# Where SiLU, sigmoid, relu and the squares stand in a group's stage, and a PSUM tile for each output step

## The chip, the cores and the metric

The kernel runs on one core of a Trainium2 chip. The metric is device microseconds (us) of one execution. Before the change the median of three runs is 1040.14 us (1040.02 to 1041.37).

## The reference

One layer of a hybrid trunk, with model width D = 1024, 512 tokens and 16 meta tokens ahead of them (L = 528):

```python
u = rmsnorm(h, mix_norm_w)
proj = u @ w_in                       # pooling, z, x/B/C, dt, gates
gate_pool, gate_ssd = sigmoid(proj[gates] + b_gate)
y_pool = pool_mixer(u_pool, pool_w_group, pool_scale) @ w_pool_up
# mamba2_branch, per group of 4 heads:
xbc = silu(conv4(xbc)); y = ssd_chunked(x, dt, a, B, C) + x * d_skip
y = y * silu(z)
y = y * rsqrt(mean(y * y over the group's 256 channels) + eps) * norm_w
y_ssd = y @ w_ssd_out
h = h + (gate_pool * y_pool + gate_ssd * y_ssd) @ w_o
v = rmsnorm(h, mlp_norm_w); h = h + relu(v @ w_ff1) ** 2 @ w_ff2
out = rmsnorm(h, final_norm_w)
```

The state-space branch has 8 groups of 4 heads, a head dimension of 64, a state of 128 and chunks of 128 tokens.

## The kernel before

All products keep fp32 accuracy by splitting each operand into a high and a low part: three matmuls per product (`mm3`, L99 to L101; the projections the same on L157, L158 and L160). Weights are streamed in blocks of 128 x 1024. For each block SP issues a load into `raw` (L74, three buffers), ScalarE (ACT) casts the high part `whi` (L75) and VectorE (DVE) subtracts to get the low part `wlo` (L76). `block()` returns the next block after it has issued this work for the blocks up to two further ahead, so a cast and a subtraction stand in the engines' queues at the place where the program asked for a block, two blocks before it is used.

The stages are: norm and first projections (to about 66 us), the groups' stage (to about 501 us), then pooling, gates, the output product W_o and the MLP. The change lies in the groups' stage, a loop over the 8 groups, in which PE, ACT and DVE run their instructions in the order in which the program writes them.

A group's cycle runs `Scan` for group g, interleaved with four steps of matmuls for the next group (`steps`): its projections B, C, x0, x1, each followed on ACT and DVE by a convolution over four taps (one pass on ACT, L347, three on DVE, L350). For group 4 the steps are instead eight output steps (`out_half`, tiles `pso`, copied to `acc` by ACT at L590), over the first eight of the normed outputs `ys`; group 4's own four projections come after them. For group 7 they are eight output steps `out_part` (tiles `psp`, added to `acc` by DVE, L598). The parts of a scan, in order:

- turn: transposes of B (tile `ptb`, L424), of x's meta tokens (`ptm`, L433) and of x (`ptx`, L444) on PE; from them ACT makes `bm` and `btok` (L428 to L430) and DVE `xdm`, `xm`, `xdt`, the low part of `bm` (L449) and `xdd` (L450);
- spread: `eb`, an Exp on ACT (L457); spans: four relus per head on `abc` (L463); decays: Exp on half of `abc` (L468);
- states: products `pcb` (L475) and `pst` (L482, L484), and the recurrence over chunks on DVE;
- scores: `abc` times `cbm` on DVE (L493); outputs: `po` (L503) and `py` (L509);
- gather: `yt` from `po`, `py`, x and z's SiLU `zt` on DVE;
- squares: Square on ACT (L522), the sum of two halves on DVE (L523), and high and low part of it (L249, L250); norm: `png` (L529); root: Ln and Exp on ACT (L533, L534); finish: `yt` scaled on DVE (L539), its high part on ACT (L542), its low part on DVE (L543).

After the scan come the next group's z in two halves (`z_half`, tile `pz`), the SiLUs of B, C and x (L354) and of z (L672), and, after groups 1, 2, 3 and 6, the product of one further pooling gate (`gate_pool`, tile `pgp`) and its sigmoid (L556). PSUM has a pool of two tiles of two banks each, used in turn by `px`, `pz`, `pgp`, `pso` and `psp`, and a pool of four single banks for the scan's small products. A tile can be taken again once its last reader is done. ACT holds one table set of functions at a time, and an `ACT_TABLE_LOAD` stands where the set changes: Ln, Exp, SiLU and sigmoid follow one another with loads between them.

Of the kernel before, what the change touches and what calls it, by code (L numbers as in the profile page):

```python
# [11 lines left out]
AF = mybir.ActivationFunctionType  # L12
ALU = mybir.AluOpType
# [3 lines left out]
SEQ = 512  # L17
NM = 16
L = SEQ + NM
HALF = L // 2  # L20
NK = D // P
# [14 lines left out]
V_MIX, V_BG, V_PS, V_CW, V_CB, V_DS, V_SN, V_MN, V_DTB, V_AL = (  # L36
    0, 8, 24, 32, 160, 192, 208, 224, 232, 233)
# [14 lines left out]
def kernel(ctx: ExitStack, tc, xT, x, w, vec, fnw, out):  # L52
    nc = tc.nc
    act, dve, pe, pool = nc.scalar, nc.vector, nc.tensor, nc.gpsimd
# [26 lines left out]
    def block():  # L81
        prepare(depth[0] + 1)
        return ahead.pop(0)[2:]

    def prepare(n):
        while len(ahead) < n:
            ahead.append(block_tiles())
            block_part(ahead[-1], slice(0, 1024))
# [32 lines left out]
    def col(off, i, n=P):  # L121
        return vs[:n, off + i : off + i + 1]
# [22 lines left out]
    m1 = [m1p.tile([P, SEQ], F32, tag=f"m1_{d}", name=f"m1_{d}") for d in range(NK)]  # L145

    def psum2(name):
        return psa.tile([P, 1024], F32, tag="mm", name=name)

    def psum1(name):  # L150
        return psb.tile([P, 512], F32, tag="s", name=name)

    def proj_step(outs, k, wblk, rhs):

        wh, wl = (t[:, k * P : (k + 1) * P] for t in wblk)
        for o, c in outs:
            pe.matmul(o, wh, rhs[0][k][:, c], start=k == 0, stop=False)  # L157
            pe.matmul(o, wh, rhs[1][k][:, c], start=False, stop=False)  # L158
        for o, c in outs:
            pe.matmul(o, wl, rhs[0][k][:, c], start=False, stop=k == NK - 1)  # L160

    def proj(outs, wblk, rhs):
        for k in range(NK):
            proj_step(outs, k, wblk, rhs)
# [8 lines left out]
    def narrow(ps):  # L173
        return [(ps, slice(NM, L))]
# [8 lines left out]
    rsb = pre.tile([P, L], F32, name="rsb")  # L183
    q = pre.tile([P, L], F32, name="q")
    X, U = (xh, xl), (uh, ul)
# [81 lines left out]
    for t, name in ((rsh, "dgh"), (rsl, "dgl")):  # L267
        d = pre.tile([NT, 6, NT], F32R, tag="sq", name=name, bufs=2)
# [84 lines left out]
    def silu(t):  # L353
        act.activation(t, t, AF.Silu)  # L354

    def group_tiles(g):
        xc = gc.tile([P, 2, L], F32, tag="xc", name=f"xc{g}")
        bt = gc.tile([P, L], F32, tag="bt", name=f"bt{g}")
        ct = gc.tile([P, SEQ], F32, tag="ct", name=f"ct{g}")
        zt = gc.tile([P, 2, SEQ], F32, tag="zt", name=f"zt{g}", bufs=1)  # L360
        return xc, bt, ct, zt
# [28 lines left out]
    def xbc_tile(g, cur, n):  # L390
        dst, t, skip = tiles_of(g, cur)[n]
        runs, view = wide(psum2(f"px{g}_{t}"), skip)
        proj(runs, block(), U)
        return lambda: conv(dst, view, t)

    def z_half(ps, i, between=None):
        wblk = block()
        for k in range(NK):
            if k == 2 and between:
                between()  # L400
            proj_step(narrow(ps[:, i * SEQ : (i + 1) * SEQ]), k, wblk, U)
# [146 lines left out]
    flat = lambda t: t.rearrange("p r d -> p (r d)")  # L548


    def gate_pool(d, first=False):
        ps = psum2(f"pgp{d}")[:, :SEQ]
        proj(narrow(ps), block(), X if first else U)
        if first:
            dve.tensor_tensor(m1[d], ps, rsb[:, NM:], op=ALU.mult)
        act.activation(m1[d], m1[d] if first else ps, AF.Sigmoid, bias=col(V_BG, d))  # L556


    cur = group_tiles(0)
    first_group(cur)  # L560
    for d in range(GATES_FIRST):
        gate_pool(d, True)
    depth[0] = 2
    prepare(2)
    norm_u()
# [11 lines left out]
    def ssd_out(d, ps, ks):  # L577
        wh, wl = block()
        for n, k in enumerate(ks):
            c = slice(n * P, (n + 1) * P)  # L580
            mm3(ps, (wh[:, c], wl[:, c]), ys[k], n == 0, n == len(ks) - 1)

    half = {}

    def out_half(d):
        if d % 2 == 0:
            half[0] = psum2(f"pso{d}")
        ps = half[0][:, (d % 2) * SEQ : (d % 2 + 1) * SEQ]
        ssd_out(d, ps, range(8))
        return lambda: act.copy(acc[d], ps)  # L590

# [2 lines left out]
    def out_part(d):  # L594
        ps = psum2(f"psp{d}")[:, :SEQ]
        for k in range(8, 14):
            mm3(ps, next(part), ys[k], k == 8, k == 13)
        return lambda: dve.tensor_tensor(acc[d], acc[d], ps, op=ALU.add)  # L598

    def scan_with(sc, steps):  # L600
        sc.turn()
        after = steps[0]()
        sc.spread()
        sc.spans((0, 1))
        after()
        sc.states()
        after = steps[1]()
        sc.decays(0)
        sc.spans((2,))
        after()  # L610
        after = steps[2]()
        sc.spans((3,))
        sc.decays(1)
        sc.scores(0)
        sc.scores(1)
        after()
        sc.outputs()
        after = steps[3]()
        sc.gather(0)
        if len(steps) > 4:  # L620
            after()
            after = steps[4]()
        sc.gather(1)
        if len(steps) > 4:
            sc.squares()
        after()
        if len(steps) > 4:
            steps[5]()()
            sc.norm()
            after = steps[6]()  # L630
            sc.root()
            after()
            after = steps[7]()
            sc.finish()
            after()

    with tc.manual_schedule(engines={mybir.EngineType.PE, mybir.EngineType.Activation, mybir.EngineType.DVE}):
        for g in range(G):
            sc = Scan(g, cur)
            if g + 1 == G:  # L640
                scan_with(sc, [lambda d=d: out_part(d) for d in range(NK)])
                break
            nxt = group_tiles(g + 1)
            tiles = [lambda n=n: xbc_tile(g + 1, nxt, n) for n in range(4)]
            if g == 4:
                scan_with(sc, [lambda d=d: out_half(d) for d in range(NK)])
                for t in tiles:
                    t()()
            else:
                scan_with(sc, tiles)  # L650
            gate = GATE_AT.get(g)
            xc, bt, ct, zt = nxt
            ps = psum2(f"pz{g + 1}")
            z_half(ps, 0)

            def silus():
                for t in (bt, ct, xc.rearrange("p i t -> p (i t)")):
                    silu(t)

            if g == 4:  # L660
                silus()
                z_half(ps, 1)
            else:
                sc.squares()
                if gate is None:
                    silus()
                z_half(ps, 1, sc.norm)
                sc.root()
                sc.finish()
                if gate is not None:  # L670
                    silus()
            act.activation(zt.rearrange("p i t -> p (i t)"), ps, AF.Silu)  # L672
            if gate is not None:
                gate_pool(gate)
            cur = nxt
    depth[0] = 0
    gc_stack.close()
# [49 lines left out]
    def gate_ssd(d):  # L727
        ps = psum1(f"pgs{d}")
        proj(narrow(ps), block(), U)
        gt = gtp.tile([P, SEQ], F32, tag="gt", name=f"gs{d}")  # L730
        act.activation(gt, ps, AF.Sigmoid, bias=col(V_BG, NK + d))
        return gt
# [4 lines left out]
    for d in range(NK):  # L737
        ps = psum2(f"psl{d}")[:, :SEQ]
# [4 lines left out]
    for n, gi in enumerate(POOL_ORDER):  # L743
        nxt = []
        if n < 3:
            nxt.append(pool_tile(2 * POOL_ORDER[n + 1]))
        if n == 0:
            gate_pool(NK - 1)
        if n == 3:
            gts = [gate_ssd(MERGE[0])]  # L750
        if n == 2:
            wgb = block()
        pool_mix(gi, pend, wgb)
        if n < 3:
            nxt.append(pool_tile(2 * POOL_ORDER[n + 1] + 1))
        pend = nxt
# [79 lines left out]
    first = []  # L836
    for n, d in enumerate(MERGE):
# [6 lines left out]
        ps = psum2(f"pup{d}")[:, :SEQ]  # L844
# [303 lines left out]
    for t in range(4):  # L1148
        T, st = t // 2, slice((t % 2) * P, (t % 2 + 1) * P)
        n = 0  # L1150
        for half in range(2):
            parts = [(0, 512)] if half == 0 or t < 3 else [(0, 256), (256, 256)]
            for a, m in parts:
                ps = p2v[t] if T == 0 and half == 0 else lastp[:, 512:] if a else (
                    lastp[:, :512] if (t, half) == (3, 0) else psum1(f"pl{t}_{half}"))
                ps = ps[:, a : a + m]
                i = 0
                for k, seg in ((1, (A11, 3)[T]), (0, (A12, A22)[T])):
                    wh, wl = wq[k, half]
                    for p in range(2):  # L1160
                        x0 = p * 512 + a
                        f = i == 0 and not (T == 0 and half == 0)
# [152 lines left out]
```

## Time and profile before

| | us |
|---|---|
| median of three runs | 1040.14 |
| the profiled execution | 1041.51 |
| its span | 1039.8 |
| its mean granted TensorE clock | 0.993 of full speed |
| groups' stage, about | 66 to 501 |

A row of the waits names the engine and tile that waited, the line, the engine and line that ended the wait, and then the total, the number and the longest wait in us. A row of the windows gives a stretch of the span in us, its length, the busy time of PE, of its weight loads, of DVE, ACT and POOL (instructions in brackets), the granted clock of PE, the DMA share and GB/s. A row of the timeline gives start, length, engine, line, operation, output and inputs, and in square brackets how long the engine had been idle and what ended that. In the chain that ended last a row has start, length, engine, tile and line. A row of the DMA issues ends with the us from issue to landing. A row of a tile gives its instructions by count, min/median/max ns and the first and the last start.

### The profile page before, as it was taken

To read this page: it belongs to the slowest core of one execution; us is meant where nothing else is said; L and a number is where in the kernel's file an instruction comes from. 1 tells how busy PE (TensorE), PEld (TensorE's weight loads), DVE (VectorE), ACT (ScalarE), POOL (GpSimd) and SP (SyncE) were. 2 spreads that over 40 slices of the span, in tenths; PEclk is the share of its full clock that TensorE was granted. 3 is DMA by queue.
4 is the path that set the end of the run, shared out by engine and by line. 5 is a ranking of instruction groups with operands and counts; after the bars stand their busy time and mean duration, and the time that the engine had idled before them with its cause. 6 is when DMAs were issued, how large, how long until landed. Compare 5 with 4: busy or idle time off the path is not lost.

```text
span 1039.8 us, 14039 instructions
## 1 busy us (share of the span) xinstructions
PE 1012.1 (97%) x5689; PEld 875.9 (84%) x5689; DVE 711.3 (68%) x894; ACT 559.9 (54%) x789; POOL 88.6 (9%) x52
## 2 busy tenths in 40 slices
PE   9999999999889999999999999999999999999997
PEld 8889889898678998978899888888888888888886
DVE  7979585858453486767757457885777666666866
ACT  7774949494734467575344333465455344454444
POOL 0100000000000000000000000101231412403400
PEclk9999999999999999999999999999999999999999
DMA  6233131414232322322723332414323323234112
GB/s 235 81 124 110 53 124 59 142 42 142 61 105 78 102 83 80 122 61 81 238 87 101 102 102 71 152 55 169 101 81 122 101 83 120 88 115 116 44 44 82
DMA packets 29282, 105.64 MB, mean 102 GB/s; under 512 B 3296, under 2 KB 4256, under 8 KB 28192
## 3 DMA queue, kind: packets, MB, share of 16 engines
q1 hardware_dynamic: 26496, 92.75, 27.7%
q0 software_dynamic: 2000, 11.08, 2.9%
q8 instruction: 45, 0.74, 0.3%
q10 hardware_dynamic: 720, 0.91, 0.2%
q14 instruction: 21, 0.17, 0.1%
HBM read 102.55 MB, written 2.16 MB: 101 GB/s over the span
## 4 chain that ended last, share of the span: by engine, by line
PE 75%; DVE 12%; ACT 10%; issue 1%; DMA 0%; SPq 0%; DVEq 0%; ACTq 0%
PE pf L100 6%; PE pf L101 6%; PE pf L99 6%; PE alpha L1064 3%; PE alpha L1065 3%; PE alpha L1066 3%; PE px L157 3%; PE px L158 3%; PE px L160 3%; DVE wlo L76 2%; PE pp L157 1%; PE pp L160 1%; PE pp L158 1%; PE pgs L160 1%; PE pup L101 1%
## 5 line engine op out<-in xcount | busy, mean ns | idle before, releaser
L76 DVE TENSOR_TENSOR wlo<-raw,whi 128x1024 fp32r<-128x1024 f32 (+1 forms) x131 | 163.8, 1252 | 127.4 <-ACT whi L75 127.4
L75 ACT CAST whi<-raw 128x1024 fp32r<-128x1024 f32 (+1 forms) x131 | 136.2, 1041 | 126.6 <-PE pf L100 55.8
L157 PE MATMUL px<-uh,whi 128*128 128x264 f32 (+1 forms) x448 | 121.1, 291 | 0.0
L158 PE MATMUL px<-ul,whi 128*128 128x264 f32 (+1 forms) x448 | 118.0, 285 | 0.0
L99 PE MATMUL pf<-vh,whi 128*128 128x512 f32 x256 | 99.8, 390 | 0.0
L101 PE MATMUL pf<-vh,wlo 128*128 128x512 f32 x256 | 99.6, 389 | 0.0
L100 PE MATMUL pf<-vl,whi 128*128 128x512 f32 x256 | 99.6, 389 | 0.0
L160 PE MATMUL px<-uh,wlo 128*128 128x264 f32 (+1 forms) x448 | 90.9, 284 | 0.0
L157 PEld LDWEIGHTS px<-uh,whi 128*128 128x128 f32 x448 | 85.6, 191 | 1.3 <-issue 1.0
L158 PEld LDWEIGHTS px<-ul,whi 128*128 128x128 f32 x448 | 85.1, 190 | 0.3
L826 DVE TENSOR_TENSOR slo<-b,shi 128x1024 fp32r<-128x1024 f32 x35 | 49.2, 1405 | 31.6 <-ACT shi L825 27.4
L160 PEld LDWEIGHTS px<-uh,wlo 128*128 128x128 f32 x448 | 69.2, 189 | 0.0
L825 ACT CAST shi<-b 128x1024 fp32r<-128x1024 f32 x35 | 36.8, 1051 | 47.3 <-PE pf L100 36.4
L99 PEld LDWEIGHTS pf<-vh,whi 128*128 128x128 f32 x256 | 48.1, 188 | 10.0
L101 PEld LDWEIGHTS pf<-vh,wlo 128*128 128x128 f32 x256 | 48.1, 188 | 10.0
L100 PEld LDWEIGHTS pf<-vl,whi 128*128 128x128 f32 x256 | 48.1, 188 | 9.9
L1075 POOL TENSOR_TENSOR b<-b,b 128x1024 f32<-128x1024 f32 x14 | 35.6, 2540 | 238.4 <-DVE slo L826 238.4
L1064 PE MATMUL alpha<-shi,hh 128*128 128x512 f32 x140 | 54.6, 390 | 0.0
L1066 PE MATMUL alpha<-shi,hl 128*128 128x512 f32 x140 | 54.5, 389 | 0.0
L1065 PE MATMUL alpha<-slo,hh 128*128 128x512 f32 x140 | 54.5, 389 | 0.0
L891 DVE TENSOR_TENSOR ht<-ht,alpha 128x1024 f32<-128x1024 f32 x35 | 42.6, 1217 | 10.9 <-PE alpha L1066 10.9
L347 ACT ACTIVATE xc<-px,vs 128x528 f32<-128x528 f32 x14 | 11.1, 791 | 70.9 <-PE px L160 70.9
(415 smaller groups left out, 2519.3 us busy)
## 6 DMA issues: line engine op xcount, KB each, us to landing
raw<-in_w SPq DMA_DIRECT2D x129, 512.0 KB, 3.6
b<-in_w SPq DMA_DIRECT2D x28, 512.0 KB, 3.5
abc<-acs_d POOLq DMA_DIRECT2D x8, 1024.0 KB, 5.3
wob<-in_w SPq DMA_DIRECT2D x8, 512.0 KB, 5.4
xt<-in_xT SPq DMA_DIRECT2D x8, 264.0 KB, 5.6
ht<-in_x POOLq DMA_DIRECT2D x4, 512.0 KB, 6.0
w<-in_w SPq DMA_DIRECT2D x4, 512.0 KB, 3.6
out_dram<-out SPq DMA_DIRECT2D x4, 320.0 KB, 2.4
```

Of the source, the lines that this page charges most:

```text
L75: act.copy(hi[:, c], raw[:, c])
L76: dve.tensor_tensor(lo[:, c], raw[:, c], hi[:, c].bitcast(F32), op=ALU.subtract)
L99: pe.matmul(ps, ah, bh, start=first, stop=False)
L100: pe.matmul(ps, ah, bl, start=False, stop=False)
L101: pe.matmul(ps, al, bh, start=False, stop=last)
L157: pe.matmul(o, wh, rhs[0][k][:, c], start=k == 0, stop=False)
L158: pe.matmul(o, wh, rhs[1][k][:, c], start=False, stop=False)
L160: pe.matmul(o, wl, rhs[0][k][:, c], start=False, stop=k == NK - 1)
L826: dve.tensor_tensor(lo, src, hi.bitcast(F32), op=ALU.subtract)
L1064: pe.matmul(ps[t], a[0], wh[:, cs], start=f, stop=False, skip_group_check=True)
L1065: pe.matmul(ps[t], a[0], wl[:, cs], start=False, stop=False, skip_group_check=True)
L1066: pe.matmul(ps[t], a[1], wh[:, cs], start=False, stop=l, skip_group_check=True)
```

## The change

Six things change, all in the groups' stage.

1. The squares of a group are issued in the scan directly behind the last convolution; before, they stood behind z's first half, or in groups 4 and 7 ahead of a step's copy.
2. The SiLUs of B, C and x always stand ahead of z's second half's products in the program; before, in the groups with a gate, they stood behind finish.
3. z's SiLU: in groups with a gate it stands directly behind z's second half, ahead of Ln, Exp and finish; in the others it is put on the list `held` and issued in the next scan behind its turning.
4. The gate's sigmoid is held in the same way. Its product stays where it was on PE.
5. The eight relus of heads 0 and 1 go from behind `eb` to behind the states and step 1's matmuls.
6. Each output step `out_half` takes a PSUM tile of its own; before, two steps shared one, each with one bank. In groups 4 and 7 the last step's copy or addition stands ahead of finish.

The diff:

```diff
-    def gate_pool(d, first=False):
+    def gate_product(d, rhs=U):
         ps = psum2(f"pgp{d}")[:, :SEQ]
-        proj(narrow(ps), block(), X if first else U)
-        if first:
-            dve.tensor_tensor(m1[d], ps, rsb[:, NM:], op=ALU.mult)
-        act.activation(m1[d], m1[d] if first else ps, AF.Sigmoid, bias=col(V_BG, d))
+        proj(narrow(ps), block(), rhs)
+        return ps
...
-    half = {}
-
     def out_half(d):
-        if d % 2 == 0:
-            half[0] = psum2(f"pso{d}")
-        ps = half[0][:, (d % 2) * SEQ : (d % 2 + 1) * SEQ]
+        ps = psum2(f"pso{d}")[:, :SEQ]
         ssd_out(d, ps, range(8))
         return lambda: act.copy(acc[d], ps)
...
+    held = []
+
     def scan_with(sc, steps):
         sc.turn()
         after = steps[0]()
+        while held:
+            held.pop()()
         sc.spread()
-        sc.spans((0, 1))
         after()
         sc.states()
         after = steps[1]()
+        sc.spans((0, 1))
         sc.decays(0)
         sc.spans((2,))
         after()
...
         sc.gather(1)
-        if len(steps) > 4:
-            sc.squares()
         after()
+        sc.squares()
         if len(steps) > 4:
             steps[5]()()
             sc.norm()
             after = steps[6]()
             sc.root()
             after()
-            after = steps[7]()
+            steps[7]()()
             sc.finish()
-            after()
...
             z_half(ps, 0)
-
-            def silus():
-                for t in (bt, ct, xc.rearrange("p i t -> p (i t)")):
-                    silu(t)
-
-            if g == 4:
-                silus()
-                z_half(ps, 1)
+            for t in (bt, ct, xc.rearrange("p i t -> p (i t)")):
+                silu(t)
+            z_half(ps, 1, None if g == 4 else sc.norm)
+
+            def z_silu(zt=zt, ps=ps):
+                act.activation(zt.rearrange("p i t -> p (i t)"), ps, AF.Silu)
+
+            if gate is not None:
+                z_silu()
+                pg = gate_product(gate)
             else:
-                sc.squares()
-                if gate is None:
-                    silus()
-                z_half(ps, 1, sc.norm)
+                held.append(z_silu)
+            if g != 4:
                 sc.root()
                 sc.finish()
-                if gate is not None:
-                    silus()
-            act.activation(zt.rearrange("p i t -> p (i t)"), ps, AF.Silu)
             if gate is not None:
-                gate_pool(gate)
+                held.append(lambda d=gate, pg=pg: act.activation(m1[d], pg, AF.Sigmoid, bias=col(V_BG, d)))
             cur = nxt
```

The gates outside this stage do what they did (product, then sigmoid). What the order of instructions shows at three places:

On ACT at the end of group 2's cycle, from Ln to the end of the SiLUs (`rs` is root's tile, `yh` finish's high part, `bt`, `ct`, `xc` and `zt` group 3's B, C, x and z), before:

```order
L533 ACT_TABLE_LOAD
L533 ACTIVATE rs_2190<-png_2169,eps 128x512
L534 ACT_TABLE_LOAD
L534 ACTIVATE rs_2190<-rs_2190 128x512
L542 CAST yh_0_2194<-yt_2023 128x512
L542 CAST yh_1_2199<-yt_2023 128x512
L354 ACT_TABLE_LOAD
L354 ACTIVATE bt_1763<-bt_1763 128x528
L354 ACTIVATE ct_1764<-ct_1764 128x512
L354 ACTIVATE xc_1762<-xc_1762 128x1056
L672 ACTIVATE zt_1765<-pz_2119 128x1024
L75 CAST whi_2209<-raw_2208 128x1024
```

The same stretch after the change, on ACT:

```order
L354 ACTIVATE bt_1762<-bt_1762 128x528
L354 ACTIVATE ct_1763<-ct_1763 128x512
L354 ACTIVATE xc_1761<-xc_1761 128x1056
L75 CAST whi_2161<-raw_2160 128x1024
L661 ACTIVATE zt_1764<-pz_2126 128x1024
L75 CAST whi_2196<-raw_2195 128x1024
L533 ACT_TABLE_LOAD
L533 ACTIVATE rs_2225<-png_2172,eps 128x512
L534 ACT_TABLE_LOAD
L534 ACTIVATE rs_2225<-rs_2225 128x512
L542 CAST yh_0_2229<-yt_2023 128x512
L542 CAST yh_1_2234<-yt_2023 128x512
```

The four SiLUs and the gate block's cast have moved from behind finish's casts to ahead of Ln.

On ACT directly behind that, group 3's turning and its first steps (`m_4` is the gate, `abc` the spans' tile, `st_3` the first state), before:

```order
L556 ACT_TABLE_LOAD
L556 ACTIVATE m_4_126<-pgp_2207,vs 128x512
L428 CAST bm<-ptb_2248 16x128
L429 CAST bm<-ptb_2248 16x128
L430 COPY btok_2247<-ptb_2248 128x384
L75 CAST whi_2280<-raw_2279 128x1024
L457 ACT_TABLE_LOAD
L457 ACTIVATE eb_2333<-abc_2239 64x1024 x2
L463 ACTIVATE abc_2239<-abc_2239,dtok 128x128 x8
L347 ACTIVATE bt_2242<-px_20_2278,vs 128x528
L486 COPY st_3_2355<-pst_0_2359 128x256
L75 CAST whi_2374<-raw_2373 128x1024
```

And after the change, the same place on ACT:

```order
L428 CAST bm<-ptb_2247 16x128
L429 CAST bm<-ptb_2247 16x128
L430 COPY btok_2246<-ptb_2247 128x384
L75 CAST whi_2279<-raw_2278 128x1024
L672 ACT_TABLE_LOAD
L672 ACTIVATE m_4_126<-pgp_2194,vs 128x512
L457 ACT_TABLE_LOAD
L457 ACTIVATE eb_2333<-abc_2238 64x1024 x2
L347 ACTIVATE bt_2241<-px_20_2277,vs 128x528
L486 COPY st_3_2347<-pst_0_2351 128x256
L75 CAST whi_2366<-raw_2365 128x1024
L463 ACTIVATE abc_2238<-abc_2238,dtok 128x128 x8
```

The sigmoid with its load has moved from ahead of the turning's copies to behind the next cast, and the eight relus from ahead of the first convolution pass to behind the state's copy and a cast.

On PE in group 4, from the end of output step 0 to the first matmul of step 1 (`yh3_1` is the last of the normed outputs used, `wlo37` and `whi38` blocks of weights, `xdd4` and `btok4` made by the turning), before:

```order
L101 MATMUL pso0_2757<-yh3_1_2678,wlo37_2638 128x512
L475 MATMUL pcb4_2800<-ct4_2243,bt4_2242 128x128 x4
L482 MATMUL pst4_0_2811<-xm_115,bm_114 128x256
L484 MATMUL pst4_0_2811<-xdd4_2754,btok4_2726 128x256
L484 MATMUL pst4_1_2812<-xdd4_2754,btok4_2726 128x256 x2
L99 MATMUL pso0_2757<-yh0_0_1271,whi38_2688 128x512
```

After the change, the same place on PE:

```order
L101 MATMUL pso0_2756<-yh3_1_2713,wlo37_2641 128x512
L475 MATMUL pcb4_2792<-ct4_2242,bt4_2241 128x128 x4
L482 MATMUL pst4_0_2803<-xm_115,bm_114 128x256
L484 MATMUL pst4_0_2803<-xdd4_2753,btok4_2725 128x256
L484 MATMUL pst4_1_2804<-xdd4_2753,btok4_2725 128x256 x2
L99 MATMUL pso1_2816<-yh0_0_1271,whi38_2675 128x512
```

The order is the same; step 1's first matmul writes `pso1` where it wrote into the second half of `pso0`.

More of the change, by code (lines that the diff above doesn't have):

```diff
@@ L548, with gate_first @@
     flat = lambda t: t.rearrange("p r d -> p (r d)")
-    def gate_pool(d, first=False):
+    def gate_product(d, rhs=U):
         ps = psum2(f"pgp{d}")[:, :SEQ]
-        proj(narrow(ps), block(), X if first else U)
-        if first:
-            dve.tensor_tensor(m1[d], ps, rsb[:, NM:], op=ALU.mult)
-        act.activation(m1[d], m1[d] if first else ps, AF.Sigmoid, bias=col(V_BG, d))
+        proj(narrow(ps), block(), rhs)
+        return ps
+    def gate_first(d):
+        ps = gate_product(d, X)
+        dve.tensor_tensor(m1[d], ps, rsb[:, NM:], op=ALU.mult)
+        act.activation(m1[d], m1[d], AF.Sigmoid, bias=col(V_BG, d))
     cur = group_tiles(0)
@@ L561 @@
     for d in range(GATES_FIRST):
-        gate_pool(d, True)
+        gate_first(d)
     depth[0] = 2
@@ L747 @@
         if n == 0:
-            gate_pool(NK - 1)
+            pg = gate_product(NK - 1)
+            act.activation(m1[NK - 1], pg, AF.Sigmoid, bias=col(V_BG, NK - 1))
         if n == 3:
```

## Prediction

> **What bounds the kernel now.** I read the page's head first, then the waits of TensorE, then the windows in which its clock falls, and last the timeline of a group.
>
> ```profile
> span 1039.8 us, 14039 instructions
> PE 1012.1 (97%) x5689; PEld 875.9 (84%) x5689; DVE 711.3 (68%) x894; ACT 559.9 (54%) x789; POOL 88.6 (9%) x52
> PE pso L99 <- ACT acc L590: 7.0, 3, 3.3
> PE py L509 <- DVE abc L493: 3.9, 4, 1.1
> PE pst L482 <- DVE bm L449: 3.3, 2, 1.6
> PE ptm L433 <- ACT xc L354: 2.4, 4, 0.6
> PE pst L484 <- DVE xdd L450: 1.9, 3, 0.6
> PE png L529 <- DVE qlg L250: 0.9, 4, 0.2
> ```
>
> PE is busy for 97%, so a change that leaves its matmuls alone can win only PE's waits and what they cause. The six rows (us in total, times, longest) are all in the groups' stage; their sum is 7.0 + 3.9 + 3.3 + 2.4 + 1.9 + 0.9 = 19.4 us. They cause something more:
>
> ```profile
> 120.81:124.22 3.41, 3.41 (x16) 3.23 (x15) 0.00 (x0) 3.36 (x8) 0.00 (x0) 0.50 0.45 154
> 277.82:281.23 3.41, 3.41 (x10) 2.62 (x9) 3.11 (x6) 2.60 (x6) 0.00 (x0) 0.50 0.00 0
> 308.54:311.95 3.41, 3.41 (x9) 2.65 (x8) 1.23 (x1) 0.36 (x1) 0.00 (x0) 0.50 0.11 24
> 410.94:414.35 3.41, 1.74 (x13) 1.36 (x11) 3.22 (x8) 3.36 (x7) 0.00 (x0) 1.00 0.00 0
> 414.35:417.76 3.41, 2.80 (x7) 2.29 (x8) 1.60 (x2) 3.35 (x4) 0.00 (x0) 0.50 0.16 24
> ```
>
> The first number after the length is PE's busy time, the 0.50 or 1.00 the granted clock. Four windows ran at half clock, in groups 1, 4 (twice) and 6, and did 1.7 us of work in 3.41: each costs about 1.6. The one at 414.35 followed a window in which PE was busy for 1.74 of 3.41 us.
>
> An undisturbed group is group 0; against it stands group 2, whose turning follows a gate's product:
>
> ```profile
> 66.44 0.49 PE L424 MATMUL ptb<-ident,bt 128*128 128x128 f32 x3
> 74.79 1.46 PE L484 MATMUL pst<-xdd,btok 128*128 128x256 f32 x6
> 89.50 1.97 PE L509 MATMUL py<-abc,xdt 128*64 128x128 f32 x32
> 108.71 0.49 PE L424 MATMUL ptb<-ident,bt 128*128 128x128 f32 x3
> L157 PE MATMUL pgp<-uh,whi x8: 389/389/389, 157.3 to 162.1; 128*128 128x512 f32 x8
> 162.78 0.49 PE L424 MATMUL ptb<-ident,bt 128*128 128x128 f32 x3
> 163.85 1.00 ACT L672 ACTIVATE zt<-pz 128x1024 f32<-128x1024 f32 x1
> 214.38 1.00 ACT L672 ACTIVATE zt<-pz 128x1024 f32<-128x1024 f32 x1
> ```
>
> From a turning PE needs 8.35 us to the states (74.79 - 66.44), 23.06 to py and 42.27 to the next turning. A gate's product adds 5.44 (157.34, in the timeline, to 162.78), so 47.71 is a gate group without a wait. Group 2's cycle, from zt to zt, takes 50.53: 2.8 too long. The waits in it are ptm 0.6, py 1.0 and png 0.2; the other 1.0 is slower matmuls behind them.
>
> **The change part by part.** PE's instructions keep number and order; only the PSUM tile of every second output step is another. Table loads on ACT stay 46. So everything is a shift of ACT and DVE work, and the sum is over PE's waits.
>
> *A gate group (2 and 3).* Before, silus of bt, ct and xc stand behind finish, and xc's ends after PE wants it (ptm). Now they stand in z's second half, so ptm's wait goes. What is late next is finish, since z's SiLU now stands ahead of Ln. The rows for its chain:
>
> ```profile
> 154.37 0.69 ACT L533 ACTIVATE rs<-png,eps 128x512 f32<-128x512 f32 x1
> 156.37 0.63 ACT L534 ACTIVATE rs<-rs 128x512 f32<-128x512 f32 x1
> 157.04 0.75 DVE L539 SCALAR_TENSOR_TENSOR yt<-yt,vs,rs 128x512 f32<-128x512 f32 x1 [2.72 <-ACT rs L534]
> 160.53 0.69 DVE L543 TENSOR_TENSOR yl<-yt,yh 128x512 fp32r<-128x512 f32 x1 [0.69 <-ACT yh L542]
> 164.75 1.03 ACT L75 CAST whi<-raw 128x1024 fp32r<-128x1024 f32 x1
> 165.80 1.28 ACT L556 ACT_TABLE_LOAD   x1
> 167.10 0.69 ACT L556 ACTIVATE m<-pgp,vs 128x512 f32<-128x512 f32 x1
> 166.96 0.41 DVE L434 TENSOR_TENSOR xdm<-ptm,decm 16x256 f32<-16x256 f32 x1
> 170.11 0.96 DVE L450 TENSOR_TENSOR xdd<-xdt,dec 128x768 f32<-128x768 f32 x1
> 465.25 0.97 DVE xdd L450
> 466.36 1.53 PE pst L484 x6
> ```
>
> Count from the end of z's product, which is the gate product's start. z's SiLU starts at about 0.2; the cast + 0.90 (163.85 to 164.75), the table load + 1.05, Ln + 1.30 (like 165.80 to 167.10): 3.45. Exp + 2.00 (154.37 to 156.37), yt + 0.67, last yl + 3.49 and 0.61 for itself: 10.2. From xdm to xdd 3.15: 13.4; the states' product 1.11 behind (465.25 to 466.36): 14.5. PE is there at 5.44 + 8.35 = 13.8. A new wait of **0.7**, then.
>
> The scores come after. ACT ends the last yh at 9.6; the turning's small copies (an estimate: 1.0) and the next cast (1.03) go to 11.6, and two loads (1.28 each) with the held sigmoid (0.69) put eb at 14.9:
>
> ```profile
> 170.94 2.14 ACT L457 ACTIVATE eb<-abc 64x1024 f32<-64x1024 f32 x2
> 173.10 2.45 ACT L463 ACTIVATE abc<-abc,dtok 128x128 f32<-128x128 f32 x8
> 176.27 2.37 DVE L350 SCALAR_TENSOR_TENSOR bt<-px,vs,bt 128x527 f32<-128x527 f32 x3 [4.06 <-ACT bt L347]
> 183.04 2.32 DVE L350 SCALAR_TENSOR_TENSOR ct<-px,vs,ct 128x512 f32<-128x512 f32 x3
> 186.40 2.35 DVE L493 TENSOR_TENSOR abc<-abc,cbm 128x1024 f32<-128x1024 f32 x2
> ```
>
> Without the eight relus (2.45, moved behind the states) bt's conv starts on ACT 2.16 after eb, at 17.0, and DVE's passes 0.8 later, as 173.10 + 2.45 stands to 176.27. The scores come 10.13 behind those (186.40 - 176.27): 28.0, their first half at 29.1. PE wants it at 5.44 + 23.06 + 0.7 = 29.2. So py's wait goes or shrinks to 0.25. The relus are hidden in C's step: between 17.0 and DVE's turn to ct's conv (6.77 behind bt's, at 24.6) ACT now has bt's pass 0.8, st's copy 0.4 (an estimate), a cast 1.0, eight relus 2.45, an Exp of a cast's size, 1.1, four relus 1.2 and ct's pass 0.7, together 7.65, to 24.65: no slack. If that cover is gone, each 0.1 missing there is 0.1 of py's wait. Squares sooner make png's wait go. Cycle: 47.71 + 0.7 + 0.1 = 48.5; gain 2.0 each, **3.9** for both. At the bounds: no new wait 2.8 each; or, if each of the three hand-overs on the new chain costs another 0.6 (ptm's wait), 0.2 each.
>
> *Entry groups (1 and 6: their turning follows a group without a gate).*
>
> ```profile
> 118.83 0.36 PE L482 MATMUL pst<-xm,bm 80*128 80x256 f32 x1 [1.65 <-DVE bm L449]
> ```
>
> Here finish was already ahead of z's SiLU, which was not in the chain that ends in bm; holding it gains nothing there. The squares' adding goes ahead of one wlo on DVE, and a cast ahead of the silus on ACT; the two are of a size (1.2 and 1.03) and nearly cancel, so I take 0.2 sooner: bm's wait 1.45 instead of 1.65, xdd's 0.6 as before. PE's busy time in that window rises by 0.2, and a 1.74 was still followed by half clock, so I leave the half clock. py 1.0 and png 0.2 go, with 0.7 of slow matmuls behind them (the share of group 2). Gain 2.1 each, **4.2**. Bounds: 0 if neither goes, 3.7 if the half clock goes as well.
>
> *Group 4.* Output steps of even number owned a tile of two banks, odd ones its second half. The first matmul of step 1 waits until step 0's bank has been copied, and that copy stands behind eb and the eight relus:
>
> ```profile
> 277.13 0.50 PE L99 MATMUL pso<-yh,whi 128*128 128x512 f32 x1 [3.04 <-ACT acc L590]
> ```
>
> With two such tiles and one per step, step 1 needs only the tile freed by the held sigmoid at 13.6, and PE asks for it at 5.44 + 8.35 + 1.5 = 15.3; step 2 needs acc 0's copy, which has a whole step of time. So pso's 7.0 go, with two half clocks (3.3, at 277.82 and 308.54), 0.4 of restarts and ptm's 0.6; against it stands the new wait at the states, here 0.6 to 1.0. Gain **10.7**; bounds 3.4 (only half the waits and no clock) and 11.5.
>
> *Group 5* has neither a gate ahead nor one behind: 0. *Group 7*, behind gate 6: its output steps are 4.2 us where a projection is 5.9, so the turning's DVE work is due sooner. I get a wait for bm of 1.35 and for xdd of 0.6, with slow matmuls behind them 2.4; the trace has one of ptm (0.6) and one of xdd (0.6), with theirs 1.8: **-0.6**, and -2.2 with a half clock. All later stages: 0, as no wait stands in the list there.
>
> *Queues.* SP issues one raw load ahead of another in one place; raw loads land in 3.6 us:
>
> ```profile
> raw<-in_w SPq DMA_DIRECT2D x129, 512.0 KB, 3.6
> ```
>
> A block is prepared two steps (over 10 us) ahead, so this cover holds. POOL's queue is unchanged.
>
> Sum: 3.9 + 4.2 + 10.7 - 0.6 = 18.2. From the profiled execution's 1041.5 that gives 1023.3; it lies 1.4 above the median, so I take 1023.0.
>
> **The rivals.**
> (a) *No half clock is left.* If bm's wait of 1.45 no longer trips the gate, the entry groups give 3.2 more less what group 7 loses, and 1021.1 comes out, or less. For it: a wait of 0.2 less. Against: the window with 1.74 busy tripped it. The Trainium skill ("TensorE: Matmul & The Clock Gate", section "HAM oscillation — how this bites in real kernels") says that only idle gaps of PE above about 3.4 us throttle it; by that rule no wait here could, and this trace disagrees: the longest wait is 3.3 and one of 1.65 did.
> (b) *The output steps still wait*, because the tile they get is held by something else (the sigmoid's, psp's or pp's); the change then doesn't do what it says in group 4. 1023.3 + 10.7 = 1034. For it: the held sigmoid frees its tile only 1.7 before PE asks. Against: each later tile has a step of time.
> (c) *The chain behind z's SiLU is longer than added up*, by x, in the four groups behind a gate (2, 3, 4, 7). Up to x = 0.5 it costs 4x = 2 us. From x = 1 the wait reaches 1.7 and trips the half clock: 4 x (1.0 + 1.6) = 10.4, so 1033; x = 2 gives 1037. For it: every hand-over in my chain is read from another place in the trace. Against: nine of ten terms are rows.
> (d) *Equal.* If each of the two loads between z's SiLU and Exp keeps ACT for a second load's time, as they now follow work without a gap, x = 2 x 1.28 = 2.6: 4 x (2.6 + 1.6) = 16.8, so 1040. Against: the load at 165.80 follows a cast without a gap, and its user starts 1.30 later. The Trainium skill ("ScalarE: Activation LUTs", section "What ACT_TABLE_LOAD costs") gives 1283 ns for a load and 1380 ns more for a drain; by that, (d) would hold, and these rows show no second part.
> (e) *Slower.* The cast between z's SiLU and Ln reads a raw block; if its load has not landed, Ln, finish, the turning and the states stand behind it, in the same four groups. x is then what is missing of the load; it decides from 4 x (x + 1.6) = 18.2, x = 2.95. At x = 3.6, the whole row of a load, 4 x 5.2 = 20.8: 1044. For it: nothing but the queue; against: loads are two steps ahead. The same price comes from any cause that makes ACT's and DVE's loop the bound, whose margin is only about 0.5 us a group.
>
> **How the numbers follow.** Forecast 0.57 (own range 1021.5 to 1025), (a) 0.13, (b) 0.05, (c) 0.10, (d) 0.04, (e) 0.11. Differences under 0.2%, 2 us, can hardly be told from none by a measurement here. Faster: 0.57 + 0.13 + 0.05 + 0.10 = 0.85; same 0.04; slower 0.11. To leave out no more than 2 in 10 the range goes from (a) with its bound for the unknown, 1019, to (b) and half of (c), 1034.
>
> **What would show it.** In the profile after: no pso wait on acc; ptm, py and png gone or below 1 us together; new waits of pst on xdd, some 0.7 four times; two windows at half clock, in groups 1 and 6. Group 2's zt-to-zt period of 48.5. Wrong if pst waits above 1.7 stand in groups 2, 3 and 4, or if pso waits for something.

## The result, and the profile after

The changed kernel takes 1023.5 us (median of four, 1022.52 to 1023.78) against 1040.09: a ratio of 0.9836, 95% interval 0.9819 to 0.9853. Forecast were 1023.0 us and a range of 1019 to 1034. The profiled execution took 1022.52 us with a span of 1020.8, 19.0 below that of before.

The head of the page, and the waits of TensorE in the groups' stage, changed kernel:

```profile
span 1020.8 us, 14036 instructions
PE 1003.9 (98%) x5689; PEld 873.6 (86%) x5689; DVE 712.3 (70%) x894; ACT 561.5 (55%) x789; POOL 88.7 (9%) x52
```

```profile
PE pst L482 <- DVE bm L449: 4.4, 3, 1.5
PE pst L484 <- DVE xdd L450: 3.6, 6, 0.6
PE py L509 <- ACT abc L468: 0.4, 1, 0.4
PE py L509 <- ACT whi L75: 0.2, 1, 0.2
```

pso's 7.0, ptm's 2.4 and png's 0.9 are gone and py's 3.9 is 0.6. What stands in their place are states that wait for the turning's work on DVE: 5.2 us in all before, 8.0 now. PE's busy time fell by 8.2 us with the same 5689 matmuls: a matmul at half clock counts as a longer one (0.63 us at 278.01 in the trace before, 0.39 at 283.17), and so does one just behind a wait.

From turning to turning (first `ptb` of each group in PE's timeline; for group 7 up to the first `pp`) the cycles are:

| group | before, us | after, us | gain | forecast |
|---|---|---|---|---|
| 0 | 42.27 | 42.27 | 0 | 0 |
| 1 | 54.07 | 50.84 | 3.2 | 2.1 |
| 2 | 50.55 | 48.63 | 1.9 | 2.0 |
| 3 | 50.53 | 48.63 | 1.9 | 2.0 |
| 4 | 97.73 | 87.01 | 10.7 | 10.7 |
| 5 | 42.27 | 42.27 | 0 | 0 |
| 6 | 54.09 | 51.98 | 2.1 | 2.1 |
| 7 | 43.31 | 44.09 | -0.8 | -0.6 |

Group 2's new chain, from the changed kernel's timeline. First DVE and ACT (the first two rows are the start of finish and the first instruction of the turning behind it), then PE; a row of PE with a bracket names the wait:

```profile
160.08 0.75 DVE L539 SCALAR_TENSOR_TENSOR yt<-yt,vs,rs 128x512 f32<-128x512 f32 x1 [2.72 <-ACT rs L534]
164.17 0.41 DVE L434 TENSOR_TENSOR xdm<-ptm,decm 16x256 f32<-16x256 f32 x1
167.32 0.96 DVE L450 TENSOR_TENSOR xdd<-xdt,dec 128x768 f32<-128x768 f32 x1
168.70 2.14 ACT L457 ACTIVATE eb<-abc 64x1024 f32<-64x1024 f32 x2
181.83 2.35 DVE L493 TENSOR_TENSOR abc<-abc,cbm 128x1024 f32<-128x1024 f32 x2
```

```profile
159.38 0.38 PE L424 MATMUL ptb<-ident,bt 128*128 128x128 f32 x2
168.43 0.89 PE L484 MATMUL pst<-xdd,btok 128*128 128x256 f32 x3 [0.53 <-DVE xdd L450]
208.01 0.49 PE L424 MATMUL ptb<-ident,bt 128*128 128x128 f32 x3
```

The gate's product began 5.44 ahead of the turning, at 153.94. Counted from there xdd starts at 13.4 (forecast 13.4), the states' product at 14.5 (14.5), eb at 14.8 (14.9), the scores at 27.9 (28.0).

The clock's windows at the two waits of 1.5 us for bm that groups 1 and 6 keep (columns: stretch, length, busy time of PE, PEld, DVE, ACT, POOL, granted clock, DMA share, GB/s), changed kernel:

```profile
117.45:120.86 3.41, 1.77 (x8) 1.48 (x9) 2.92 (x4) 3.37 (x4) 0.00 (x0) 1.00 0.00 0
120.86:124.27 3.41, 3.41 (x30) 3.41 (x29) 1.18 (x2) 3.36 (x6) 0.00 (x0) 1.00 0.55 154
...
393.96:397.37 3.41, 1.24 (x8) 0.85 (x7) 3.32 (x6) 3.38 (x3) 0.00 (x0) 1.00 0.00 0
397.37:400.78 3.41, 3.41 (x14) 3.03 (x13) 0.80 (x2) 3.35 (x6) 0.00 (x0) 0.50 0.47 150
```

The waits are the same, 1.52 and 0.64 in group 1 against 1.54 and 0.63 in group 6; in group 6 they fall into one window and half clock follows, in group 1 a piece of them lies outside it and none follows. That is the 1.1 us between the two rows of the table.

### The profile page after: what moved, and what is told of

The parts are those of the page before. It is cut to its first block, busy times and chain, and to the rows that moved or that the text cites. A ratio compares the mean times of both kernels' runs of the same rounds, so it can differ in the third digit from the quotient of the medians.

```text
span 1020.8 us, 14036 instructions
## 1 busy us (share of the span) xinstructions
PE 1003.9 (98%) x5689; PEld 873.6 (86%) x5689; DVE 712.3 (70%) x894; ACT 561.5 (55%) x789; POOL 88.7 (9%) x52
## 4 chain that ended last, share of the span: by engine, by line
PE 84%; ACT 9%; DVE 6%; issue 1%; DMA 0%; SPq 0%; ACTq 0%
PE pf L100 6%; PE pf L99 6%; PE pf L101 6%; PE px L157 5%; PE px L158 5%; PE px L160 5%; PE alpha L1063 3%; PE alpha L1064 3%; PE alpha L1065 3%; PE pz L160 2%; PE pz L157 2%; PE pz L158 2%; PE py L509 2%; PE pp L160 2%; PE pp L157 1%; ACT whi L75 1%
## 5 line engine op out<-in xcount | busy, mean ns | idle before, releaser
L347 ACT ACTIVATE xc<-px,vs 128x528 f32<-128x528 f32 x14 | 11.1, 790 | 62.3 <-PE px L160 62.3
```

## The experiments

Open is which of the six edits the 16.6 us come from, and whether the new wait at the states is what is left. Unless it says "the kernel before", an experiment is the changed kernel with one edit (e9: with two). Each was timed beside the kernel before; the times are medians of four executions, with the ratio to the kernel before. Beside the different experiments the kernel before had medians of 1040.97 to 1041.98 us, so a difference of about 1 us to the changed kernel's 1023.5 shows nothing.

**e1: the tile alone.** The kernel before with

```diff
-        if d % 2 == 0:
-            half[0] = psum2(f"pso{d}")
-        ps = half[0][:, (d % 2) * SEQ : (d % 2 + 1) * SEQ]
+        ps = psum2(f"pso{d}")[:, :SEQ]
```

> The kernel before with one change only: each output step has its PSUM tile. Theory (the tile alone carries group 4's gain of 10.7 us: three pso waits of 7.0 in all, two windows at half clock 3.3, 0.4 of slow matmuls): no pso wait, half clocks in groups 1 and 6 only, 1040.1 - 10.7 = 1029.4 us. Rival (the copies also had to come sooner, behind fewer relus): half of the pso waits stay, 1034 or more.

1030.75 us, ratio 0.9894 (0.9879 to 0.9909). Three rows of the waits of the kernel with the tile alone:

```profile
PE py L509 <- DVE abc L493: 3.9, 4, 1.1
PE ptm L433 <- ACT xc L354: 2.5, 4, 0.6
PE px L157 <- DVE bt L350: 1.2, 1, 1.2
```

No wait for `acc` is left; the others in the stage, those for bm, xdd and qlg too, stand as before within 0.1. Group 4's cycle is 86.64 (350.70 - 264.06) where it was 97.73: 11.1 us. The tile carries group 4's gain, and the places of relu and SiLU are not needed for it. In group 1 no half clock occurred in this execution, and still its cycle is 54.06 (162.98 - 108.92) where it was 54.07 with one: PE waited 1.2 for px instead, for which e3 gives the cause. So in the kernel before, the half clock in group 1 cost nothing.

**e2: the old sharing of tiles in the changed kernel.** The same lines the other way round.

> The changed kernel with the old sharing of a PSUM tile by two output steps. Theory: with the relus moved, step 0's copy stands directly behind eb, at about 17.5 us from the gate product's start where PE asks at 15.9, so 1.7 us of wait instead of 3.0, the later ones shorter than 3.3 and 0.7 too: 1023.5 + 3 to 5 = 1027 to 1028.5 us. Rival (the tile alone decides, the order of ACT does not matter): all of 10.7 comes back, 1034 us.

1027.48 us, ratio 0.9861 (0.9846 to 0.9875). In this kernel's waits stands

```profile
PE pso L99 <- ACT acc L593: 2.9, 3, 1.5
```

so three waits, of 1.5 and twice 0.7, in place of 3.0, 3.3 and 0.7. The theory holds in size: with the other edits in, sharing a tile costs 4 us and not 10.7. Two of the waits shrink. At the first, step 0's copy stands directly behind eb, without the eight relus between (2.44 us in the trace before). The second shrinks by the squares' place, which the theory does not have. On ACT the kernel before had the Square and the cast of the sum, which waits for DVE, ahead of the copy; in the kernel with the shared tile the copy comes first, at 295.26. ACT's timeline before:

```profile
306.85 0.62 ACT L249 CAST qhg<-sqg 128x512 fp32r<-128x512 f32 x1 [0.76 <-DVE sqg L523]
307.37 0.58 ACT L590 COPY acc<-pso 128x512 f32<-128x512 f32 x1
```

The edits overlap in group 4; their gains can't be added.

**e3: the relus back.**

```diff
         sc.spread()
+        sc.spans((0, 1))
         after()
         sc.states()
         after = steps[1]()
-        sc.spans((0, 1))
```

> The changed kernel with the eight relus back behind eb. Theory (the chain from eb to the scores is within 0.2 us of PE in groups 2 and 3): py waits of about 2.3 us in groups 2 and 3, 1 to 2 in 1, 6 and 7, some of them tripping the half clock: 1030 to 1034 us. Rival (the relus were covered, DVE's own queue sets the scores): 1023.5 us.

1030.95 us, ratio 0.9897 (0.9881 to 0.9914). Two rows of the waits of the kernel with the relus back:

```profile
PE py L509 <- DVE abc L493: 4.8, 5, 1.1
PE px L157 <- DVE bt L350: 4.2, 4, 1.2
```

The relus are worth 7.4 us, and the theory's size fits, but its place only half: PE loses 0.9 to 1.2 already at x0's projection, because its PSUM tile is B's and B's convolution, 2.45 later, still reads it; then 1.1 at py. In the profiled execution no half clock occurred in the stage.

**e4: the order inside finish.**

```diff
             for i in range(2):
                 y = self.yt[:, i, :]
                 dve.scalar_tensor_tensor(y, y, col(V_SN, 2 * self.g + i), self.rs, op0=ALU.mult, op1=ALU.mult)
+            for i in range(2):
+                y = self.yt[:, i, :]
                 yh = yp.tile([P, SEQ], F32R, tag="yh", name=f"yh{self.g}_{i}")
```

> The changed kernel with finish's two scalings issued one after the other, ahead of the two casts and subtractions, so that DVE no longer idles 0.69 us twice in the chain from Exp to the turning. Theory (finish's chain is what the states wait for): the chain ends 1.35 us sooner, pst waits fall by that in groups 1, 6 and 7 and vanish in 2, 3 and 4 (in all 5.7 us), no half clock in the stage: 1015 to 1017 us. Rival (ACT's loop is the bound, the wait moves on to py): 1020 us or more.

1014.67 us, ratio 0.9739 (0.9725 to 0.9754). Finish and what follows it on DVE in the kernel with the other order of finish, timeline, and then that kernel's waits in the groups' stage:

```profile
158.81 1.42 DVE L539 SCALAR_TENSOR_TENSOR yt<-yt,vs,rs 128x512 f32<-128x512 f32 x2 [2.72 <-ACT rs L534]
160.26 1.35 DVE L545 TENSOR_TENSOR yl<-yt,yh 128x512 fp32r<-128x512 f32 x2
161.53 0.41 DVE L434 TENSOR_TENSOR xdm<-ptm,decm 16x256 f32<-16x256 f32 x1
```

```profile
PE pst L484 <- DVE xdd L450: 1.9, 3, 0.6
PE py L509 <- ACT whi L75: 0.4, 2, 0.2
PE py L509 <- ACT abc L468: 0.4, 1, 0.4
PE pst L482 <- DVE bm L449: 0.2, 1, 0.2
```

From the first scaling to xdm it is 2.72 us (158.81 to 161.53) where the changed kernel needs 4.09 (160.08 to 164.17), as DVE there idles 0.69 twice until the cast on ACT is done. The states' waits fall from 8.0 to 2.1 and groups 2 and 3 reach their bound: 205.83 - 158.12 = 47.71, a gate group without a wait.

```profile
158.12 0.38 PE L424 MATMUL ptb<-ident,bt 128*128 128x128 f32 x2
205.83 0.38 PE L424 MATMUL ptb<-ident,bt 128*128 128x128 f32 x2
```

So what the changed kernel still waited for in these groups was the length of finish's chain, and not ACT's load as a whole.

**e5: the four SiLUs behind finish again**, in the groups with a gate:

```diff
-            for t in (bt, ct, xc.rearrange("p i t -> p (i t)")):
-                silu(t)
+            if gate is None:
+                silus()
             z_half(ps, 1, None if g == 4 else sc.norm)
...
-            if gate is not None:
-                z_silu()
-                pg = gate_product(gate)
-            else:
+            if gate is None:
                 held.append(z_silu)
             if g != 4:
                 sc.root()
                 sc.finish()
+            if gate is not None:
+                silus()
+                z_silu()
+                pg = gate_product(gate)
```

> The changed kernel with all four SiLUs behind finish again in the groups with a gate (squares sooner, sigmoid held, relus late, own tiles stay). Theory (moving them exchanges ptm's wait of 0.6 for the states' wait of 0.5 to 0.6, and costs group 7 its wait for bm of 1.3): no pst wait in groups 2, 3 and 4, ptm waits of 0.6 four times, 1022 to 1024 us, equal. Rival (the SiLUs' place carries the 2 us that groups 2 and 3 each won): 1027.5 us or more.

1020.11 us, ratio 0.9795 (0.9773 to 0.9817): better than the changed kernel by 3.4, more than either theory had, and on the far side from the rival. Its waits:

```profile
PE pst L482 <- DVE bm L449: 3.1, 2, 1.5
PE ptm L433 <- ACT xc L354: 2.0, 4, 0.8
PE pst L484 <- DVE xdd L450: 1.9, 3, 0.6
```

ptm's waits are back, but two of the four are below 0.2, and no state waits in groups 2, 3 and 4; the cycles of 2, 3, 4 and 7 are 48.78, 48.04, 86.19 and 43.29, together 2.1 us less than in the table. Moving the SiLUs ahead of finish, in these groups, took from the kernel and gave it nothing; the 1.9 us that groups 2 and 3 won each came from the other edits. In this profiled execution no half clock occurred in the stage, but the clock makes little of the 3.4: at the same mean clock of 0.995, an execution of this kernel took 1020.6 us and two of the changed kernel 1023.3 and 1023.71.

**e6: z's SiLU alone behind finish.**

```diff
-            if gate is not None:
-                z_silu()
-                pg = gate_product(gate)
-            else:
+            if gate is None:
                 held.append(z_silu)
             if g != 4:
                 sc.root()
                 sc.finish()
+            if gate is not None:
+                z_silu()
+                pg = gate_product(gate)
```

> The changed kernel with z's SiLU alone behind finish in the groups with a gate; the other SiLUs stay in z's second half. Theory (Ln can start only at 1.0 us after z's product, the first yt scaling to the last yh take to 7.2, a table load and the SiLU to 9.4; the tile of z is the one that the next projection takes, at 6.9): px waits for zt by about 2.5 us in groups 2, 3 and 4 and psp in 7, with some half clocks, so 1032 to 1037 us. Rival (finish ahead of it only removes the states' wait): 4 waits of 0.5 to 2 us go, 1020 us.

1025.32 us, ratio 0.9844 (0.9826 to 0.9862). Waits, and ACT's timeline in group 1's end, of the kernel with z's SiLU behind finish:

```profile
PE pst L482 <- DVE bm L449: 3.1, 2, 1.5
PE px L157 <- ACT zt L661: 2.8, 2, 1.5
PE psp L99 <- ACT zt L661: 2.4, 1, 2.4
PE pst L484 <- DVE xdd L450: 1.9, 3, 0.6
...
PE pso L99 <- ACT zt L661: 1.5, 1, 1.5
```

```profile
160.81 0.62 ACT L542 CAST yh<-yt 128x512 fp32r<-128x512 f32 x1 [1.42 <-DVE yt L539]
161.44 1.28 ACT L661 ACT_TABLE_LOAD   x1
162.74 1.02 ACT L661 ACTIVATE zt<-pz 128x1024 f32<-128x1024 f32 x1
```

The mechanism is the forecast one, a PSUM tile held by z's SiLU, and it replaces the states' wait; its size was wrong. zt ended 8.4 us after z's product (155.31, 5.44 ahead of 160.75), where 9.4 were forecast, since Ln started with the end of z's product and not 1.0 behind it; so the waits were 1.4 to 1.5 in groups 2, 3 and 4 and not 2.5. In group 7 it was 2.4, about as forecast. In the profiled execution a half clock followed none of them. With the states' waits gone against that, the net is 2 us slower than the changed kernel and not 8.5 or more.

**e7: the sigmoid not held.**

```diff
-                held.append(lambda d=gate, pg=pg: act.activation(m1[d], pg, AF.Sigmoid, bias=col(V_BG, d)))
+                act.activation(m1[gate], pg, AF.Sigmoid, bias=col(V_BG, gate))
```

> The changed kernel with the gate's sigmoid directly behind finish, ahead of the turning's copies. Theory (the table load and the sigmoid, 2.0 us on ACT, stand ahead of copies whose readers on DVE come only 1.5 us or more later, and eb starts at the same time): same time within 1 us, 1023.5 us. Rival (the copies for bm come 2.0 us later and so the states): pst waits of 2.0 to 2.5 us in groups 2, 3, 4 and 7 with half clocks, 1035 us or more.

1023.04 us, ratio 0.9822 (0.9803 to 0.9842): as the theory had it. The waits are those of the changed kernel (bm 4.4 in three, xdd 3.6 in six). Holding it costs and brings nothing that these times show.

**e8: the squares late.**

```diff
         sc.gather(1)
-        after()
-        sc.squares()
         if len(steps) > 4:
+            sc.squares()
+        after()
+        if len(steps) > 4:
...
             z_half(ps, 0)
+            if g != 4:
+                sc.squares()
```

> The changed kernel with the squares behind z's first half again (in groups 4 and 7 ahead of a step's copy). Theory (only DVE's subtraction comes ahead of the squares' sum, ACT's order behind it hardly shifts): png waits of 0.2 come back, bm's wait in groups 1 and 6 grows by about 0.15, 1024.5 us. Rival (the squares' place carries what the groups 1 and 6 won, 2.1 us each): 1027.5 us.

1026.56 us, ratio 0.9854 (0.9832 to 0.9877): 3.1 slower than the changed kernel, beyond the theory's 1.0 and near the rival's sum, though not by its mechanism. PE's timeline in group 2, squares late:

```profile
199.19 0.39 PE L160 MATMUL pz<-uh,wlo 128*128 128x512 f32 x1
199.55 0.50 PE L529 MATMUL png<-qhg,ones_r 128*128 128x512 f32 x1
200.28 0.50 PE L529 MATMUL png<-qlg,ones_r 128*128 128x512 f32 x1 [0.23 <-DVE qlg L250]
200.61 0.39 PE L157 MATMUL pz<-uh,whi 128*128 128x512 f32 x1
```

The wait that this row calls 0.23 is dearer than it looks: from 199.19 to 200.61 it is 1.42 us for three matmuls that are issued every 0.23 us when nothing waits, so 0.73 is lost. Groups 2 and 3 have cycles of 49.35 and 49.34, that is 0.7 more than in the table. bm's wait grew by 0.12 only, but in the profiled execution three half clocks stood in the stage, behind groups 1, 6 and 7, where the changed kernel's had one. By these cycles the squares' place is worth about 2 us (an estimate: 0.7 in each of groups 2 and 3, and 0.2 in 1, 6 and 7, the last three set against cycles that had a half clock too: 51.96 for group 1 and 45.02 for group 7 in e7, 51.98 for group 6 in the changed kernel). The rest of the 3.1 is probably the clock's; how much in the other executions can't be said, as only one is profiled.

**e9: finish's order, and xdd in three pieces.** As e4, and

```diff
-            dve.tensor_tensor(self.xdd, xdt[:, :3, :, :], bc(dec[:, :3, hs], 64), op=ALU.mult)
+            for c in range(3):
+                dve.tensor_tensor(self.xdd[:, c, :, :], xdt[:, c, :, :], bc(dec[:, c, hs], 64), op=ALU.mult)
```

> Finish's two scalings first, as in the run of that name, and xdd made in three pieces, one for each chunk, so that the first states' product can start when 0.4 us of it is done instead of 0.96. Theory (the states' remaining wait is xdd's length): pst waits on xdd fall from 0.63 to about 0.1 in groups 1, 6 and 7, DVE has 0.3 us more per group, which nothing waits for: 1014.7 - 1.5 = 1013.2 us. Rival (PE then reaches py sooner, whose wait of 0.2 to 0.4 grows by as much): 1014.7 us.

1014.53 us, ratio 0.9742 (0.9727 to 0.9756), the same as e4. The waits with xdd in pieces:

```profile
PE py L510 <- ACT whi L75: 1.5, 2, 0.8
PE py L510 <- ACT abc L469: 0.9, 1, 0.9
```

No state waits any more, and py waits for 2.4 instead of 0.8: the rival. What ends last now does so whatever happens at the states. The rows name ACT, but in group 1 it is DVE: from B's convolution, which starts at 121.94 behind ACT's pass, DVE works without a pause of over 0.1 us to the scores (132.07, the first half done at 133.30), and py starts at 133.40. The decays' Exp for these scores had ended at 126.55. In group 7 the subtraction ahead of the scores waits for a cast that stands behind twelve relus on ACT.

**e10: z's SiLU not held** in the groups without a gate:

```diff
-            else:
-                held.append(z_silu)
             if g != 4:
                 sc.root()
                 sc.finish()
+            if gate is None:
+                z_silu()
```

> The changed kernel with z's SiLU directly behind finish in the groups without a gate (0, 4, 5), instead of held. Theory (load and SiLU are 2.3 us on ACT ahead of the copies for bm, which DVE reads 3 us later; the same work stands ahead of eb either way): same time within 1 us, 1023.5 us. Rival (holding it took 2 us from the chain of groups 1 and 6): pst waits of 3 us or more there with half clocks, 1029 us.

1022.89 us, ratio 0.982 (0.9804 to 0.9836): the theory again. The waits are those of the changed kernel.

## Why the prediction was right

*What bounds the kernel.* That only PE's waits and their half clocks could be won holds: the cycle of e4 in groups 2 and 3 is 47.71, to the hundredth the sum worked out from group 0 and a gate's product, and no gate group went below it.

*Group 4.* Right in size (10.7) and cause: e1 shows the tile alone does it. The prediction gave the gain to the tile with the copy's place as no condition; e2 shows that the other edits without the tile bring two thirds of it too (a cycle of 90.77), by the relus and by the squares, of which the prediction names only the relus.

*Gate groups 2 and 3.* The chain behind z's SiLU was met to 0.1 us at each of its four points, so rivals (c), (d) and (e) had no ground. The relus' cover held (e3: 7.4 us without it), with a slack of 0.3 where none was forecast: ACT's pass for C ends at 178.14 and DVE takes it up at 178.47. The states' wait was 0.5 where 0.7 stood; yet the cycle is 48.63, 0.92 above the bound, where 0.8 stood. A wait costs more than its row, as e8 shows, and the two misses nearly cancel: that the gain came out at 1.9 for 2.0 is in part luck.
One reason was wrong: the prediction opens these groups with the SiLUs moving into z's second half, as what removes ptm's wait. It removes it, and e5 shows that the new wait at the states is about as dear (group 2: 48.63 against 48.78) or dearer (0.6 to 0.8 in groups 3, 4 and 7); the gain came from the relus (2.3 in each of groups 2 and 3 by e3) and the squares (0.7 by e8).

*Entry groups.* Forecast were 2.1 each. Group 6 gave 2.1; group 1 gave 3.2, since its half clock did not occur. The prediction left the half clock in both, as the wait hardly shrank, and did not ask where the wait falls against the clock's windows; that term was off by 1.1 in the profiled execution. It is half of rival (a), and chance decides it: e7 and e10 have the same waits, and there groups 1 and 7 had a half clock and group 6 none. The profiled execution, with one, is the fastest of the four. The mean clocks of the other three, 0.995 to 0.996 for 0.997, fit about one more (an estimate: a window takes 3.41 x 0.5 / 1021 = 0.0017 off the mean), so the median execution probably has the two that were forecast, though perhaps not in the groups named.
The price of a half clock, 1.6, was too high. In the changed kernel it is 1.1 (51.98 against 50.84). In the kernel before, group 1's cost nothing, as PE waited that much less for px (e1). Over the 20 executions of the kernel before that were timed with the experiments, 3.3 us lie between a mean clock of 0.990 and of 0.998; that is about five windows, so 0.7 each (an estimate). The 3.3 for two half clocks in group 4's sum was then partly wait; the gain there, 10.7, came out all the same. The prices of rivals (a), (c), (d) and (e), which use 1.6, are too high as well. And rival (a)'s 1021.1 does not follow from its own terms: 1023.0 - 3.2 is 1019.8, and what group 7 loses is not worked out.

*Group 7.* -0.8 for -0.6, by the bm wait of 1.3 and the xdd wait of 0.6 that were forecast, and a wait of 0.4 at py that was not.

*Rival (b)* fell: no pso wait. *Holding* SiLU and sigmoid was costed at nothing; without it e7 and e10 are 0.5 and 0.6 us faster, inside the executions' spread (1022.52 to 1023.78).

The table load on ACT: in e6 the load begins as the cast ends (160.81 + 0.62) and its user starts 1.30 later. The Trainium skill ("ScalarE: Activation LUTs", section "What ACT_TABLE_LOAD costs") adds a drain of some 1380 ns to the load; this trace shows none on this chain.

## What to carry to other kernels

When an engine is 97% busy, work out the cycle it would have without a wait from an undisturbed stage, then follow one chain through the new order with start-to-start times of the old trace: it came out to 0.1 us here. Moving work off one chain puts it onto another, so undo each part of a bundle by itself: here the tile and the relus carried most of the gain, the squares about 2 us (more where a tile is shared, by a copy that they hold up), the held SiLU and sigmoid nothing, and the SiLUs ahead of finish cost time. And look inside the chain that remains: two lines in another order in finish brought 9 us more, as much again as half of the whole change.

## What the runs showed of the hardware

In every trace with more than one window at half clock, these windows lie on a grid of 3.413 us: in the kernel before they start at 120.81, 277.82, 308.54 and 414.35, that is 46, 9 and 31 steps apart. Laid over the groups' stage of all twelve traces, this grid has 14 windows in which PE was busy for 0.54 to 1.55 us, and the window behind each was at 0.50; none with 1.77 or more was followed by it. Between the two it is mixed: 1.74 was followed by half clock, 1.64, 1.65 and 1.73 were not. So the limit lies near half a window (1.71), and the busy time of the trace doesn't give it more closely. The grid stands differently against the program in each execution, so that the same wait of 1.5 us (with one of 0.6 behind it) trips it in one group or run and not in another. From the kernel with the shared tile, groups 7 and 4, the kernel with the tile alone, group 1, and the one with the squares late, group 1:

```profile
446.84:450.25 3.41, 1.44 (x10) 1.11 (x10) 3.30 (x6) 3.36 (x4) 0.00 (x0) 1.00 0.00 0
450.25:453.66 3.41, 3.41 (x9) 2.66 (x9) 2.66 (x5) 3.33 (x5) 0.00 (x0) 0.50 0.41 127
265.93:269.34 3.41, 1.64 (x7) 1.17 (x7) 1.82 (x3) 3.35 (x5) 0.00 (x0) 1.00 0.24 91
269.34:272.76 3.42, 3.42 (x15) 2.82 (x16) 2.96 (x7) 3.40 (x10) 0.00 (x0) 1.00 0.16 65
```

```profile
118.15:121.56 3.41, 1.89 (x9) 1.59 (x10) 2.80 (x4) 3.38 (x4) 0.00 (x0) 1.00 0.00 0
```

```profile
116.53:119.94 3.41, 1.13 (x8) 0.80 (x7) 3.30 (x6) 3.36 (x4) 0.00 (x0) 1.00 0.00 0
```

The Trainium skill ("TensorE: Matmul & The Clock Gate", section "HAM oscillation — how this bites in real kernels") has as its abstract rule no idle gaps of PE above some 3.4 us. These runs differ: waits of 1.5 and 0.6 us in one window were enough.

A short wait cost PE 0.4 to 0.5 us beyond its row: 0.73 for a wait of 0.23 in e8, 0.92 for one of 0.53 in the changed kernel. In a stream without waits a matmul's row is 0.39 us long and the next starts 0.23 behind it, so neighbours overlap by 0.16; around a wait this overlap is lost. That this is the whole reason is not shown.
